# Attention of a two-layer trunk: read-back of turned blocks, residual loads, closing normalisation and two copies moved

## The chip, the cores and the metric

The kernel runs on one core of a Trainium2 chip. The time is that of one whole execution in device microseconds. A core has five engines that work side by side, each on its own list of instructions in order: TensorE (PE in the profile, with PEld for its weight loads), VectorE (DVE), ScalarE (ACT), GpSimd (POOL) and SyncE (SP), which here issues the transfers between DRAM and the core's memory. Engines wait for one another by semaphores. Matrix products go to PSUM, from where VectorE and ScalarE fetch them; everything else lies in SBUF.

## The reference, cut to what matters

```python
def diff_attention(qkv, q_gain, k_gain, lam_params, sub_gain, lam_init):
    q, k, v = jnp.split(qkv, 3, axis=-1)                 # 8 heads, two parts r of 64 each, values of 128
    q = rms_norm(q.reshape(bsz, seq, 8, 2, 64), q_gain) * (64 ** -0.5)
    k = rms_norm(k.reshape(bsz, seq, 8, 2, 64), k_gain)
    ...
    logits = einsum('bqhrd,bkhrd->bhrqk', q_blk, k) - slopes * dist    # causal
    probs = softmax(logits)
    attn = probs[:, :, 0] - lam * probs[:, :, 1]
    o = einsum('bhqk,bkhe->bqhe', attn, v)
    ...
    o = rms_norm(o, sub_gain) * (1.0 - lam_init)

def reference(...):                                      # SEQ = D_MODEL = 1024, fp32
    for layer in range(2):
        if layer == 0: h = h + even_mixer(h)             # gMLP gate and gated delta rule
        else:          h = h + diff_attention(rms_norm(h) @ w_qkv) @ w_out
        h = h + square(relu(rms_norm(h) @ w_mlp1)) @ w_mlp2
        h = h + (p[layer] @ w_ple_proj) * sigmoid(rms_norm(h) @ w_ple_gate)
```

The change touches the attention of the second layer and the output projection behind it, and nothing else.

## The kernel before, in words

Every product is made of fp32r parts: an operand is split into a high and a low part (`hi`, `lo`), and `mm3` (L206) multiplies high by high, high by low and low by high. The tile framework puts the written program into an order for each engine by its own model of durations, readiness and priority, and sets the semaphores. `Ordered` (L44) adds to that: `behind` (L60) tells the framework to place one instruction after another, without a wait on the chip; `mark` is the name of the last matrix instruction written so far.

**Attention** (`attention`, L877). The loop at L1150 runs over 64 blocks `g` = 8 heads times 8 blocks of 128 queries, and two more turns for the rest. In turn `g` it writes `logits(0)` of block `g`, `combine` and `transpose` of block `g-1`, `logits(1)` of block `g`, and `value` of block `g-3`. Between them `pump` (L1126) takes units from the stream that projects q, k and v of the next heads (matrix products `mm`), and behind the 220th pump units of `tails` (L1137): the projected outputs of the heads that are done.

- `logits` (L1015): scores to PSUM (`qk`), VectorE adds the slopes and takes the extreme (L1029), ScalarE takes the exponential (L1032).
- `combine` (L1034): VectorE, the two probabilities into one. `transpose` (L1042): VectorE turns 32x32 squares (L1045), SP writes the block to `a_dram` (L1047) and reads it back with the squares in turned places into `aT` (L1053). The read-back must wait until the write has landed.
- `value` (L1056): `po` = the turned block times v; VectorE copies `po` to `o` (L1064), ScalarE squares it with a sum (L1066); behind every fourth block VectorE, GpSimd (L1078 to L1080) normalise four blocks of `o`, and SP writes them to `o_dram` (L1082).
- `put_q` (L985): for each of the two parts `r`, ScalarE scales 64 rows of the turned queries out of PSUM (L993), VectorE copies these to the other 64 rows (L994), and VectorE makes the low part (L995). `put_k` (L975) does the like for the keys.
- `put_o` (L1084): four outputs are turned on PE (`tr`), ScalarE makes `ohi` (L1090) and VectorE `olo` (L1091).

PSUM has tags of two buffers each: `mm`, `tr`, `aux`, `sc`. `tr` serves `put_k`, `put_q` and `put_o`; in the projection behind the attention `mm` and `tr` both take products.

**Projection.** `mix_part` (L1186) multiplies the first six (first half of the tokens) or five heads (second half) by `w_out`, one of eight tiles `m` of 128 outputs after another. It loads the residual row `res` (L1193), makes the products, adds `res` (L1199) and stores the sum in `h_dram` (L1200). `res` comes from `tmp`, a ring of four buffers of 128x512 that the squares of the attention use too. `mix_out` (L1203) does the rest with the remaining heads: load of `acc` from `h_dram` (L1214), products, sum (L1225), squares (L242, L243), store (L1227).

**Close.** The last block's `value` and the last `put_o` stand in `close` (L1179), which the caller runs at the 8th of 16 steps of `mix_out(0)` (L1950). The upper half of `acc` for the first tokens (tiles 4 to 7) lies where v of the last heads lay, so its load waits for the last `po`.

Of the kernel before, what the change touches and what calls it, by code (L numbers as in the profile page):

```python
# [39 lines left out]
def f32(ap):  # L40
    return ap.bitcast(F32)
# [73 lines left out]
class Trunk:  # L115
# [761 lines left out]
    def attention(self, w_qkv, w_out, gain_next, h_dram):  # L877
# [91 lines left out]
        def begin(hd):  # L969
# [15 lines left out]
            def put_q(b2):  # L985
                pt = self.aux([P, HT], "tr", "tr")
                for i in range(2):
                    self.pe.transpose(pt[:, i * P : (i + 1) * P], qk[0][b2 // 2][:, 2 * (b2 % 2) + i, :], self.ident)
                qh = self.slot(f"c{11 + b2 % 2}", [P, 2, 2 * P], F32R, "qh")
                ql = qlow[b2 % 2]  # L990
                for r in range(2):
                    own, other = half[r], half[1 - r]
                    nc.scalar.activation(qh[own, r], pt[own, 0 : 2 * P], AF.Copy, scale=self.qg[own])  # L993
                    nc.vector.tensor_copy(qh[other, r], f32(qh[own, r]))  # L994
                    nc.vector.scalar_tensor_tensor(ql[own, r], pt[own, 0 : 2 * P], self.qg[own], f32(qh[own, r]), ALU.mult, ALU.subtract)  # L995
                return qh, ql
# [4 lines left out]
        class Block:  # L1001
# [40 lines left out]
            def transpose(me):  # L1042
# [5 lines left out]
                src = a_dram.rearrange("k (i r) (j c) -> k (r j) i c", r=32, c=32)  # L1048
                me.aT = []
                for k0 in range(0, nk, 4):  # L1050
                    k1 = min(nk, k0 + 4)
                    aT = self.attn_tile(next(aT_tag))
                    nc.sync.dma_start(aT[:, : (k1 - k0) * P].rearrange("p (k i c) -> p k i c", i=4, c=32), src[k0:k1].rearrange("k p i c -> p k i c"))  # L1053
                    me.aT.append(aT)

            def value(me):  # L1056
# [7 lines left out]
                nc.vector.tensor_copy(o[b // 4][:, b % 4, :], po)  # L1064
# [85 lines left out]
        for g in range(8 * NB + 2):  # L1150
# [15 lines left out]
            pump()  # L1166
            if g > 2:
                blocks[g - 3].value()
# [10 lines left out]
        def close():  # L1179
            blocks[8 * NB - 1].value()  # L1180
            put_o(7, 1, os[7][1])

        return close


    def mix_part(self, h, n, w_out, h_dram):  # L1186
        nc = self.nc
        cols = slice(h * HT, (h + 1) * HT)
        for m in range(KT):
            if m % 2 == 0:  # L1190
                w = self.weight(w_out[0 : n * P, m * P : (m + 2) * P], n, 256)
            res = self.tmp()
            nc.sync.dma_start(res, h_dram[m, :, cols])  # L1193
# [684 lines left out]
def trunk(tc, x, p, ln_mix_e, w_in_e, gmlp_v_gain, gmlp_ws, gmlp_bs, gdn_conv, gdn_a_log, gdn_dt_bias, gdn_out_gain,  # L1878
          w_out_e, ln_mix_o, w_qkv_o, attn_q_gain, attn_k_gain, diff_lambda, attn_sub_gain, w_out_o, ln_mlp, w_mlp1,
          w_mlp2, ln_ple, w_ple_gate, w_ple_proj, masks, out):  # L1880
    with ExitStack() as ctx:
# [54 lines left out]
        for layer in range(2):  # L1936
# [10 lines left out]
            if layer:  # L1947
                T.new_hs()
                for n, _ in enumerate(T.mix_out(0, lambda m: acc_of(m, 0), w_out_o[0], h_dram, gain[4], KA[0])):
                    if n + 1 == 4 * (KT - KA[0]):  # L1950
                        close()
# [11 lines left out]
            close = T.attention(w_qkv_o[0], w_out_o[0], gain[4], h_dram)  # L1963
# [41 lines left out]
```

## Time and profile before

| | us |
|---|---|
| time, median of 3 runs | 2525.89 (2522.48 to 2528.98) |
| the profiled execution, its own time | 2526.67 |
| its span, first to last instruction | 2524.9 |
| mean granted TensorE clock | 0.996 |
| attention and both halves of its projection lie at | 1260 to 1800 of the span |

The profile counts from the start of the span. It gives the busy time of each engine, a table by stretch (busy us of each engine with the number of instructions, the granted TensorE clock as a share of full speed, the share of the transfer engines and GB/s), the waits by who waited for whom, and a timeline. The busy time of PE is pipelined and its ends are modelled, so a row of the timeline with an idle time and its releaser is the surest sign of a wait on PE.

### The profile page before, as it was taken

What the parts mean: (1) busy time and instruction counts of PE and PEld (TensorE: products, weight loads), DVE (VectorE), ACT (ScalarE), POOL (GpSimd) and SP (SyncE); (2) the same over time, 40 slices, a digit from 0 to 9 for tenths busy, and PEclk for the clock granted to TensorE, in tenths of its full rate; (3) what the DMA queues carried; (4) which work ended last, traced back from release to release, by engine and by line L of the source; (5) the groups of instructions that cost most, each with busy time, mean ns of one, the idle gap of its engine ahead of it and who ended that gap; (6) DMA issues with size and microseconds to landing.
All of it is one profiled execution on the core that took longest, in us unless ns stands there. A gap on an engine that the chain in (4) does not pass through costs nothing.

```text
span 2524.9 us, 39928 instructions
## 1 busy us (share of the span) xinstructions
PE 2493.6 (99%) x13758; PEld 2126.0 (84%) x13758; DVE 1899.0 (75%) x3740; ACT 1246.7 (49%) x2457; POOL 287.5 (11%) x256
## 2 busy tenths in 40 slices
PE   9999999999999999999999999999999999999999
PEld 7898898888888887888999999977788888888877
DVE  7876767587667879566588888986887677787586
ACT  6543444465455435444355555543654445445452
POOL 0211232000000000000244343300000000000000
PEclk9999999999999999999999999999999999999999
DMA  7353435447556755553346666779375558655651
GB/s 241 123 161 80 133 110 186 142 163 245 168 179 233 253 185 194 186 167 106 111 119 159 159 167 144 180 214 292 127 230 199 173 189 283 209 188 184 199 179 59
DMA packets 494531, 443.06 MB, mean 175 GB/s; under 512 B 188436, under 2 KB 361464, under 8 KB 494328
## 3 DMA queue, kind: packets, MB, share of 16 engines
q1 hardware_dynamic: 494312, 440.51, 56.8%
q8 instruction: 108, 1.77, 0.3%
q14 instruction: 95, 0.78, 0.1%
q10 hardware_dynamic: 16, 0.00, 0.0%
HBM read 312.47 MB, written 127.93 MB: 174 GB/s over the span
## 4 chain that ended last, share of the span: by engine, by line
PE 85%; DVE 8%; DMA 4%; issue 2%; SPq 1%; ACT 1%; POOL 0%; DVEq 0%; ACTq 0%; POOLq 0%
PE mm L76 75%; PE aux L76 2%; PE po L76 2%; PE qk L76 2%; DVE lg L1029 1%; DMA raw<-in_w_mlp_dram 1%; PE tr L79 1%; DVE lg L1040 1%; DVE w L224 1%; DVE lg L1045 1%; DMA raw<-in_w_ple_gate_dram 1%; DVE ks L983 0%; DVE ql L995 0%; DMA aT<-a_dram 0%; DVE ss L921 0%
## 5 line engine op out<-in xcount | busy, mean ns | idle before, releaser
L76 PE MATMUL mm<-g,w 128*128 128x512 f32 x2592 | 603.7, 394 | 0.8 <-DVE g L224 0.5
L223 ACT CAST w<-raw 128x512 fp32r<-128x512 f32 x598 | 365.7, 618 | 455.3 <-PE mm L76 370.5
L76 PEld LDWEIGHTS mm<-g,w 128*128 128x128 f32 x2592 | 485.9, 188 | 116.3 <-issue 1.1
L76 PE MATMUL mm<-hi,w 128*128 128x512 f32 x1728 | 554.6, 397 | 0.3 <-ACT hi L1240 0.3
L76 PE MATMUL mm<-w,hi 128*128 128x256 f32 (+2 forms) x2528 | 502.3, 295 | 0.9 <-DVE k L928 0.7
L224 DVE TENSOR_TENSOR w<-raw,w 128x512 fp32r<-128x512 f32 x534 | 364.3, 690 | 180.5 <-ACT w L223 176.1
L76 PEld LDWEIGHTS mm<-w,hi 128*128 128x128 f32 x2528 | 399.2, 188 | 15.1 <-PE qk L76 0.6
L76 PEld LDWEIGHTS mm<-hi,w 128*128 128x128 f32 x1728 | 325.3, 189 | 73.9 <-ACT hi L1240 0.7
L76 PE MATMUL mm<-w,lo 128*128 128x256 f32 (+2 forms) x1264 | 369.5, 293 | 0.0
L76 PE MATMUL mm<-lo,w 128*128 128x512 f32 x864 | 342.0, 396 | 0.9 <-DVE lo L1241 0.9
L76 PE MATMUL mm<-t,w 128*128 128x512 f32 x1152 | 270.9, 394 | 1.2 <-ACT w L223 1.2
L76 PEld LDWEIGHTS mm<-t,w 128*128 128x128 f32 x1152 | 216.2, 188 | 52.8 <-ACT w L223 1.6
L76 PEld LDWEIGHTS mm<-w,lo 128*128 128x128 f32 x1264 | 238.1, 188 | 6.1
L76 PEld LDWEIGHTS mm<-lo,w 128*128 128x128 f32 x864 | 163.2, 189 | 37.0 <-DVE lo L1241 1.4
L224 DVE TENSOR_TENSOR g<-graw,g 128x512 fp32r<-128x512 f32 x216 | 147.3, 686 | 8.0 <-DMA gd<-g 7.0
L223 ACT CAST g<-graw 128x512 fp32r<-128x512 f32 x216 | 132.9, 618 | 30.1 <-issue 9.3
L1032 ACT ACTIVATE lg<-lg,nm 128x128 f32<-128x128 f32 (+7 forms) x128 | 99.6, 778 | 84.1 <-DVE nm L1029 83.1
L260 POOL TENSOR_TENSOR r<-ms,mhalf 128x4 f32<-128x4 f32 x12 | 13.4, 1119 | 1043.1 <-DVE ms L258 1015.3
L350 ACT ACTIVATE g<-g 128x512 f32<-128x512 f32 x96 | 60.6, 633 | 112.5 <-DVE g L284 109.0
L224 POOL TENSOR_TENSOR w<-raw,w 128x512 fp32r<-128x512 f32 x64 | 84.6, 1337 | 99.6 <-ACT w L223 67.9
L76 PE MATMUL mm<-ohi,w 128*128 128x512 f32 x256 | 89.7, 413 | 3.9 <-DVE t L1199 2.4
L76 PE MATMUL mm<-ahi,w 128*128 128x512 f32 x256 | 82.8, 399 | 0.4 <-DVE acc L1225 0.4
(334 smaller groups left out, 3551.2 us busy)
## 6 DMA issues: line engine op xcount, KB each, us to landing
raw<-in_w_mlp_dram SPq DMA_DIRECT2D x352, 256.0 KB, 3.2
graw<-gd SPq DMA_DIRECT2D x224, 256.0 KB, 2.7
gd<-g SPq DMA_DIRECT2D x192, 256.0 KB, 3.0
raw<-in_w_ple_gate_dram SPq DMA_DIRECT2D x76, 256.0 KB, 3.0
acc<-h_dram SPq DMA_DIRECT2D x64, 256.0 KB, 4.4
keep<-in_w_mlp_dram SPq DMA_DIRECT2D x64, 256.0 KB, 4.1
raw<-in_w_in_e_dram SPq DMA_DIRECT2D x60, 256.0 KB, 3.6
h_dram<-acc SPq DMA_DIRECT2D x48, 256.0 KB, 2.6
```

What stands on the lines that cost most here:

```text
L76: self._next(self.engine.matmul(*a, **k))
L79: self._next(self.engine.transpose(*a, **k))
L223: self.nc.scalar.copy(hi, src)
L224: (lo_engine or self.nc.vector).tensor_tensor(lo, src, f32(hi), ALU.subtract)
L260: nc.gpsimd.tensor_tensor(r, ms, self.mhalf[:, 0:4], ALU.pow)
L350: nc.scalar.activation(g, src, AF.Relu)
L1029: nc.vector.tensor_tensor_reduce(out=lg[:, k0:k1], in0=ps[:, : k1 - k0], in1=al[:, u0 + k0 : u0 + k1], scale=-1.0, scalar=3.0e38 if c == 0 ...
L1032: nc.scalar.activation(lg[:, :n], lg[:, :n], AF.Exp, bias=nm[:, r, nch - 1 : nch], scale=-1.0, accum_out=me.sums[:, b, r : r + 1])
L1040: nc.vector.scalar_tensor_tensor(me.lg[1][:, :n], me.lg[1][:, :n], rs, me.lg[0][:, :n], ALU.mult, ALU.add)
L1045: nc.vector.transpose(me.lg[0][:, :n], me.lg[1][:, :n])
```

## The change

Four edits in the attention and its projection:

1. In `put_q` the copy to the other 64 rows is made by ScalarE, straight from PSUM with the same scale, in place of VectorE's copy in SBUF.
2. In `value` the copy of `po` to `o` is made by ScalarE in place of VectorE.
3. The read-back of `aT` becomes a method `fetch` that the loop calls behind `logits(1)` of the next block, and each read is placed behind the last matrix instruction written until then.
4. `mix_part` loads the residual row of tile `m+1` ahead of the products of tile `m`. `close` is split: `value` at the 8th step of `mix_out(0)`, `put_o` at the 12th.

```diff
@@ put_q @@
                     nc.scalar.activation(qh[own, r], pt[own, 0 : 2 * P], AF.Copy, scale=self.qg[own])
-                    nc.vector.tensor_copy(qh[other, r], f32(qh[own, r]))
+                    nc.scalar.activation(qh[other, r], pt[own, 0 : 2 * P], AF.Copy, scale=self.qg[own])
                     nc.vector.scalar_tensor_tensor(ql[own, r], pt[own, 0 : 2 * P], self.qg[own], f32(qh[own, r]), ALU.mult, ALU.subtract)
@@ transpose @@
-                src = a_dram.rearrange("k (i r) (j c) -> k (r j) i c", r=32, c=32)
+                me.src = a_dram.rearrange("k (i r) (j c) -> k (r j) i c", r=32, c=32)
+
+            def fetch(me):
+                nk = me.b + 1
                 me.aT = []
                 for k0 in range(0, nk, 4):
                     k1 = min(nk, k0 + 4)
                     aT = self.attn_tile(next(aT_tag))
-                    nc.sync.dma_start(aT[:, : (k1 - k0) * P].rearrange("p (k i c) -> p k i c", i=4, c=32), src[k0:k1].rearrange("k p i c -> p k i c"))
+                    self.pe.behind(nc.sync.dma_start(aT[:, : (k1 - k0) * P].rearrange("p (k i c) -> p k i c", i=4, c=32), me.src[k0:k1].rearrange("k p i c -> p k i c")), self.pe.mark)
                     me.aT.append(aT)
@@ value @@
-                nc.vector.tensor_copy(o[b // 4][:, b % 4, :], po)
+                nc.scalar.copy(o[b // 4][:, b % 4, :], po)
                 sq = self.tmp(P)
                 nc.scalar.activation(sq, po, AF.Square, accum_out=me.osq[:, b : b + 1])
@@ attention, the loop and its end @@
                 blocks[g].logits(1)
             pump()
+            if 0 < g <= 8 * NB:
+                blocks[g - 1].fetch()
             if g > 2:
                 blocks[g - 3].value()
...
-        def close():
-            blocks[8 * NB - 1].value()
-            put_o(7, 1, os[7][1])
-
-        return close
+        return blocks[8 * NB - 1].value, lambda: put_o(7, 1, os[7][1])
@@ mix_part @@
+        def load(m):
+            if m < KT:
+                res = self.tmp()
+                nc.sync.dma_start(res, h_dram[m, :, cols])
+                return res
+
+        ahead = load(0)
         for m in range(KT):
             if m % 2 == 0:
                 w = self.weight(w_out[0 : n * P, m * P : (m + 2) * P], n, 256)
-            res = self.tmp()
-            nc.sync.dma_start(res, h_dram[m, :, cols])
+            res, ahead = ahead, load(m + 1)
             ps = self.mm_ps()
@@ trunk @@
-                    if n + 1 == 4 * (KT - KA[0]):
-                        close()
+                    if n + 1 in (4 * (KT - KA[0]), 6 * (KT - KA[0])):
+                        close.pop(0)()
...
-            close = T.attention(w_qkv_o[0], w_out_o[0], gain[4], h_dram)
+            close = [*T.attention(w_qkv_o[0], w_out_o[0], gain[4], h_dram)]
```

The framework orders each engine anew. The lists below hold line, operation, what is written, what is read, and the shape; the number behind a name tells one buffer use from another.

**SP, the second call of `mix_part`, by the write of the last block (`a_dram_18841`).** The residual row of tile 4 is `t_19002` before and `t_18955` now, that of tile 5 `t_19022` and `t_19004`. Before:

```order
L101 DMA raw_19227<-in_w_out_o_dram 128x512
L1214 DMA acc_19360<-h_dram 128x512
L101 DMA raw_19342<-in_w_out_o_dram 128x512
L1214 DMA acc_19360<-h_dram 128x512
L1047 DMA a_dram_18841<-lg_12530 128x8x128
L1200 DMA h_dram<-t_18933 128x512
L101 DMA raw_19348<-in_w_out_o_dram 128x512
L1193 DMA t_19002<-h_dram 128x512
L1193 DMA t_19022<-h_dram 128x512
```

Now:

```order
L101 DMA raw_19218<-in_w_out_o_dram 128x512
L1194 DMA t_18955<-h_dram 128x512
L101 DMA raw_19342<-in_w_out_o_dram 128x512
L1222 DMA acc_19360<-h_dram 128x512 x2
L1047 DMA a_dram_18841<-lg_12530 128x8x128
L1208 DMA h_dram<-t_18883 128x512
L101 DMA raw_19348<-in_w_out_o_dram 128x512
L1194 DMA t_19004<-h_dram 128x512
```

Tile 4's load stood behind the block's write, a store and a weight load, and now stands ahead of them all; tile 5's has kept its place behind the weight load.

**PE, the close.** `po_19191` is the last value product, `tr_19212` (now `tr_19251`) the turning of the last four outputs, `mm` with `ohi_19105` or `ohi_19123` are products of `mix_out(0)`, with `ohi_18832` or `ohi_19114` of `mix_out(1)`. Before (lines left out are the further products of the same tiles):

```order
L76 MATMUL po_19191<-v_16753,aT_18845 128x128 x4
L76 MATMUL mm_19179<-ohi_19105,w_19129 128x512
...
L76 MATMUL mm_19248<-ohi_19105,w_19223 128x512
...
L76 MATMUL mm_19274<-ohi_19123,w_19230 128x512
L79 MATMUL tr_19212<-ident,o_18817 128x128 x4
L76 MATMUL mm_19235<-ohi_19105,w_19223 128x512
```

Now:

```order
L76 MATMUL po_19191<-v_16753,aT_18894 128x128 x4
L76 MATMUL mm_19226<-ohi_19105,w_19214 128x512
...
L76 MATMUL mm_19179<-ohi_19105,w_19129 128x512
...
L76 MATMUL mm_19239<-ohi_19105,w_19214 128x512
...
L76 MATMUL mm_19274<-ohi_19123,w_19221 128x512
L76 MATMUL mm_19377<-ohi_18832,w_19344 128x512
...
L76 MATMUL mm_19377<-ohi_19114,w_19351 128x512
L79 MATMUL tr_19251<-ident,o_18817 128x128 x4
```

Between the last value product and the turning stood 18 products of 512 columns (three tiles), and now stand 30 (four tiles and six products of a fifth); tile `mm_19179` starts five products later behind `po`.

**PE, the start of the last head.** `tr_18152` turns keys, `tr_18161` queries, `tr_18191` (now `tr_18187`) four outputs of an earlier head; `qk_18175` is the first score product of the head. Before:

```order
L79 MATMUL tr_18152<-ident,k_17746 128x128 x4
...
L79 MATMUL tr_18161<-ident,q_17744 128x128 x2
L76 MATMUL mm_18236<-olo_18147,w_18224 128x512
L76 MATMUL mm_18236<-ohi_18146,w_18225 128x512
L76 MATMUL qk_18175<-ks_18151,qh_18164 128x128
L76 MATMUL qk_18260<-ks_18151,qh_18164 128x256
L76 MATMUL qk_18175<-ks_18151,ql_12526 128x128
L76 MATMUL qk_18260<-ks_18151,ql_12526 128x256
L79 MATMUL tr_18191<-ident,ol_18066 128x128 x4
```

Now:

```order
L79 MATMUL tr_18152<-ident,k_17744 128x128 x4
...
L79 MATMUL tr_18161<-ident,q_17742 128x128 x2
L76 MATMUL mm_18234<-olo_18147,w_18222 128x512
L76 MATMUL mm_18234<-ohi_18146,w_18223 128x512
L76 MATMUL qk_18175<-ks_18151,qh_18164 128x128
L76 MATMUL qk_18262<-ks_18151,qh_18164 128x256
L76 MATMUL mm_18294<-ohi_18072,w_18216 128x512
...
L76 MATMUL mm_18294<-ohi_18146,w_18223 128x512
L76 MATMUL qk_18175<-ks_18151,ql_12526 128x128
L76 MATMUL qk_18262<-ks_18151,ql_12526 128x256
L79 MATMUL tr_18187<-ident,ol_18062 128x128 x4
```

The first score products stand where they stood, two products behind the queries' turning; the twelve products of `mm_18294` have moved ahead of the low parts and of the next turning of outputs.

## The prediction, made before the changed kernel ran

> **What bounds the kernel now.** I read the page's first rows, then the table by stretch around the edited stage, then the waits of PE in it, and last the timeline at the places where PE stands still. The first two rows are the page's; the rest is the table by stretch (start and end, length, busy us of PE, PEld, DVE, ACT, POOL with their instructions, granted clock, share of the transfer engines, GB/s).
>
> ```profile
> span 2524.9 us, 39928 instructions
> PE 2493.6 (99%) x13758; PEld 2126.0 (84%) x13758; DVE 1899.0 (75%) x3740; ACT 1246.7 (49%) x2457; POOL 287.5 (11%) x256
> ...
> 600.00:700.00 100.00, 100.00 (x433) 81.15 (x432) 68.19 (x108) 47.91 (x84) 0.00 (x0) 1.00 0.58 190
> 1260.00:1700.00 440.00, 431.74 (x3285) 411.55 (x3284) 386.75 (x1055) 245.26 (x601) 156.73 (x126) 0.99 0.67 161
> 1300.00:1640.00 340.00, 335.21 (x2662) 324.78 (x2661) 305.70 (x841) 191.90 (x474) 136.17 (x111) 1.00 0.68 159
> 1640.00:1660.00 20.00, 16.54 (x85) 13.34 (x84) 18.09 (x40) 11.15 (x27) 2.65 (x2) 0.83 0.78 204
> 1649.70:1656.60 6.90, 6.10 (x17) 4.91 (x18) 6.74 (x15) 2.70 (x8) 0.00 (x0) 0.51 0.68 113
> 1700.00:1704.00 4.00, 2.69 (x12) 1.49 (x10) 2.84 (x7) 1.20 (x4) 0.00 (x0) 1.00 0.98 302
> 1733.00:1736.00 3.00, 1.51 (x7) 1.19 (x7) 2.16 (x4) 0.00 (x0) 0.00 (x0) 1.00 1.01 284
> 1750.00:1761.00 11.00, 7.08 (x25) 5.58 (x26) 5.43 (x12) 2.33 (x6) 2.25 (x3) 0.84 1.05 394
> 1755.50:1759.00 3.50, 3.43 (x10) 2.90 (x11) 1.39 (x3) 0.69 (x1) 0.02 (x1) 0.51 1.06 401
> ```
>
> PE is the bound: it has something to do in 99% of the span, and in an undisturbed stretch (600 to 700) a product of 512 columns starts every 100/433 = 0.23 us. The change takes nothing from PE, so all that it can gain is the time in which PE stands still in this stage, and what the clock loses behind that. By the rows PE is idle for 340.00 - 335.21 = 4.8 us in the long attention stretch, 20.00 - 16.54 = 3.5 at the start of the last head, 1.3 and 1.5 in the projection, and 11.00 - 7.08 = 3.9 at the close: 15.0 together. Two of these places are followed by a stretch at half clock (0.51), where 6.10 us and 3.43 us of busy PE did about half of that in work: 3.0 and 1.7 lost. The whole stake is 19.7 us, 0.8% of the time.
>
> Who PE waited for in 1260 to 1800 (us in total, times, longest):
>
> ```profile
> PE tr L79 <- POOL o L1080: 2.8, 1, 2.8
> PE mm L76 <- DVE t L1199: 2.4, 2, 1.5
> PE qk L76 <- DVE qh L994: 1.9, 2, 1.4
> PE po L76 <- DMA aT<-a_dram: 1.6, 3, 0.7
> PE mm L76 <- DVE acc L1225: 1.5, 1, 1.5
> ```
>
> The names are those of the four edits: the closing normalisation (L1080), the residual sum (L1199), the query copy (L994), the read-back (`aT`). So each edit aims at a real wait; the question is how much of each it reaches.
>
> **Two copies to ScalarE.** Durations (min/median/max in ns) and, in the last two rows, what ScalarE waited for between 1260 and 1700:
>
> ```profile
> L993 ACT ACTIVATE qh<-tr,qg x64: 454/471/474, 1262.6 to 1690.4; 64x256 fp32r<-64x256 f32 x64
> L994 DVE CAST qh<-qh x64: 284/289/1358, 1263.5 to 1691.1; 64x256 fp32r<-64x256 f32 x64
> L995 DVE SCALAR_TENSOR_TENSOR ql<-tr,qg,qh x64: 435/484/493, 1263.8 to 1691.4; 64x256 fp32r<-64x256 f32 x64
> L1064 DVE COPY o<-po x64: 245/288/294, 1287.6 to 1747.6; 128x128 f32<-128x128 f32 x64
> L1066 ACT ACTIVATE t<-po x64: 257/278/283, 1290.5 to 1751.7; 128x128 f32<-128x128 f32 x64
> ...
> ACT t L1066 <- DVE o L1064: 57.6, 38, 4.1
> ACT qh L993 <- DVE ql L995: 16.4, 21, 1.6
> ```
>
> VectorE loses 64 x 0.289 + 64 x 0.288 = 37 us and falls from 386.75 to about 350 of 440; ScalarE gains 64 x 0.471 + 64 x 0.278 = 48 us and rises from 245 to 293 of 440. Neither becomes the bound by its sum. Much of the 48 us fills time that ScalarE spent waiting: 57.6 us for VectorE's copy of `po` ahead of its own square of the same tile, which now follows a copy on the same engine. For the queries the chain of one part was 0.47 + 0.29 + 0.48 = 1.24 us and becomes 0.47 + 0.47 + 0.48 = 1.42, as the low part now has both ScalarE reads ahead of it; the second part waits for the first one's low part (21 waits), so a turning takes 2.8 us in place of 2.5. Against that, the high part no longer waits in VectorE's queue, the fuller of the two. What hides the longer chain is the products between a turning and its first score product; without that cover each of the 32 turnings costs 0.36 us, 11.5 us in all.
>
> A rule of the Trainium skill speaks against these two edits: the page "ScalarE: Activation LUTs", section "Rules for kernel authors", puts plain elementwise work on VectorE and not on ScalarE. The rows agree on the length of the query copy (0.47 against 0.29), but not for `po` (0.28 against 0.29); by the rule alone the two edits would be a loss, which is the third rival below.
>
> **The read-back.** SP's own waits between 1270 and 1740, and the landing of the `aT` reads:
>
> ```profile
> SPq L1053 <- DMA a_dram<-lg: 115.3, 53, 4.4
> ...
> DMA to landing us min/median/max: 1.9/3.5/6.4
> ```
>
> SP stands for 115 us with a read at its head that waits for its own write; that is what the edit would have to open for other transfers. In the new order of SP the reads stand as near behind their writes as before (2.4 rows on average, 2.6 before): the placing behind a matrix instruction sets an order in the framework's plan and no wait, and there is little else to go between. I cost it at nothing. The cover is the two turns between a block's write and its `value`; only three products waited for `aT`, 1.6 us. Bounds: 1.6 gained, or 4 lost if some `value` that now stands nearer behind its logits meets a landing of 6.4 in place of 3.5 once or twice.
>
> For the stretch 1300 to 1640 I take, of the 4.8 us of idle PE, 0.9 gained: half of the 1.6 for `aT` and of the few tenths for `qh` there. Bounds: 4 lost (above), 4.8 gained.
>
> **The residual rows.** VectorE's waits in 1640 to 1780, its longest, and SP's issues ahead of it:
>
> ```profile
> DVE t L1199 <- DMA t<-h_dram: 16.0, 4, 7.0
> ...
> 1733.84 0.69 DVE L1199 TENSOR_TENSOR t<-t,mm 128x512 f32<-128x512 f32 x1 [6.99 <-DMA t<-h_dram]
> ...
> 1721.92 0.39 SPq L101 DMA_DIRECT2D raw<-in_w_out_o_dram  x1
> ...
> 1727.18 1.13 SPq L1193 DMA_DIRECT2D t<-h_dram  x2
> ```
>
> VectorE works in order, so while it waits 7 us for a row, the weights' low parts and sums behind it wait too. PE stood for this at 1700 to 1704 and 1733 to 1736, 1.3 + 1.5 = 2.8 us. The long one is tile 4 of the second call: its load has moved ahead of the last block's write, a store and a weight load, to a place behind the weight load that was issued at 1721.92 in place of 1727.18, 5 us earlier, which leaves about 2 of VectorE's 7 us and nothing for PE. Tile 5 has hardly moved. The loads hold a second buffer of a ring of four, so a load may now wait for the store two tiles back; a tile lasts 15 products or more (3.5 us), and the load has two tiles. I take 2.3 gained; bounds 2.8, and 1.5 lost if the ring holds a load up once.
>
> **The close.** PE, ScalarE and GpSimd from the last value product on:
>
> ```profile
> 1745.35 1.50 PE L76 MATMUL po<-v,aT 128*128 128x128 f32 x12
> 1751.15 0.50 PE L76 MATMUL mm<-ohi,w 128*128 128x512 f32 x1 [1.52 <-DVE acc L1225]
> 1755.57 1.11 PE L79 MATMUL tr<-ident,o 128*128 128x128 f32 x4 [2.76 <-POOL o L1080]
> ...
> 1751.13 0.63 ACT L242 ACTIVATE t<-acc 128x512 f32<-128x512 f32 x1 [1.20 <-DVE acc L1225]
> 1751.67 0.26 ACT L1066 ACTIVATE t<-po 128x128 f32<-128x128 f32 x1
> ...
> 1754.48 1.04 POOL L1080 TENSOR_TENSOR o<-o,of 128x512 f32<-128x512 f32 x1
> ```
>
> The last `po` ends at 1746.9, the normalised `o` at 1755.5, and PE turns it at 1755.6: 8.7 us, covered by 18 products (18 x 0.23 = 4.1 us) and 1.52 + 2.76 = 4.3 us of waiting. The chain is long because the square of `po` (1751.67) stands in ScalarE's order behind the square of an output tile (1751.13), and it still does in the new order. That tile's products now start five later (1.2 us), which the chain can bear, as VectorE reached its sum 2 us late anyway. So the chain stays 8.7 us, the cover becomes 30 products, 6.9 us, and 1.8 us of waiting are left: 2.5 gained. A lone wait of this size (1733 to 1736) left the clock at 1.00, so the 1.7 us at half clock may go too; I count half, 0.8. Together 3.3. Bounds: 5.6 (all), and 1.5 lost, if the upper `acc` rows, whose load still waits for the last `po`, hold PSUM and stop PE once more.
>
> **The start of the last head.** PE's three waits ahead of the first half-clock stretch:
>
> ```profile
> 1645.07 0.66 PE L79 MATMUL tr<-ident,k 128*128 128x128 f32 x4 [1.06 <-DVE olo L1091]
> 1648.56 0.49 PE L76 MATMUL qk<-ks,qh 128*128 128x128 f32 x2 [1.45 <-DVE qh L994]
> 1650.50 0.87 PE L79 MATMUL tr<-ident,ol 128*128 128x128 f32 x3 [0.94 <-PE qk L76]
> ```
>
> The third goes: twelve products (2.8 us) now stand ahead of that turning. The second changes its name, from VectorE's copy to ScalarE's, two products behind the turning as before; the first hangs on VectorE's queue, which is lighter by a tenth. I take 1.4 of the 3.5 us, and of the 3.0 us at half clock 1.8, as the idle time that brought it on is less than two thirds. Together 3.2; bounds 6.5, and 2 lost.
>
> On the clock a rule of the Trainium skill stands against my reading: "TensorE: Matmul & The Clock Gate", section "HAM oscillation — how this bites in real kernels", asks for gaps of PE above about 3.4 us. The trace differs, as 0.51 followed gaps of 1.06, 1.45 and 0.94. By the page no gap here would touch the clock, the 0.8 and 1.8 fall away, and the time would be 2518.8.
>
> As a mechanism of this kernel that would be half-clock stretches that come whatever the waits do. It ends inside the forecast's own range, and I give it 0.1 of the forecast's chance.
>
> **Sum.** 0.9 + 2.3 + 3.3 + 3.2 = 9.7 us. The profiled execution took 2526.67, 0.8 above the median of 2525.89; 2526.67 - 9.7 = 2517.0, and on the median's scale 2516.2.
>
> **The rivals.** First, everything that the edits aim at goes: 2.8 + 5.6 + 6.5, and 1.6 + 0.5 in the long stretch, 17.0 us, 2508.9. For it: the waits carry the edits' own names. Against: neither the 8.7 us chain nor the first score product has its cover complete.
>
> Second, the waits only change their names: the reads are not later, tile 5's load has kept its place, a turning takes longer, and the clock drops as before. What is left is 2.5 at the close and about 1.1 in the projection: 3.6 us, 2522.3. For it: SP's order by the read-backs, and transfer engines at 0.98 to 1.05 in 1700 to 1761, where a load issued earlier only queues elsewhere.
>
> Third, slower: ScalarE's order becomes the wait. Its two copies of a part stand behind exponentials and casts, and the first score product after a turning waits for `qh`, as it did once for 1.4 us at the last head. If a third to a half of the 32 turnings, say 13, lose those 1.4 us, 18 are lost against 5.6 gained in the projection and at the close: 2538. It decides from ten such turnings on (14 - 5.6 is above 7.6). Against: only 2 of 32 waited in the trace, and ScalarE is idle for a third of the stage even with the copies.
>
> **How the numbers follow.** The forecast has 0.52, its own range 2511 to 2521; first rival 0.16, second 0.21, third 0.11. A measurement of this kernel tells 0.3% (7.6 us) from no change, so faster means below 2518.3: about three quarters of the forecast (0.40) and the first rival, 0.56; same is the rest of the forecast (0.12) and the second, 0.33; slower 0.11. The range reaches from the first rival with the spread of the runs (3 us) halved, 2507, to 4 lost at the read-back with the rest at nothing, 2530; what is left out is most of the third rival and a little below.
>
> **What would show it.** Right: no wait of PE for L1080 above 2 us; VectorE's waits for residual rows at 5 us or less; no stretch of half clock behind the close, and a shorter one or none at the last head; the square of `po` waiting for no VectorE copy; SP's waits for `a_dram` near 115 us. Wrong: waits of `qk` for ScalarE's `qh` of more than 5 us; waits for `aT` above 4 us; 0.5 clock at other places of the stage; PE idle in 1300 to 1640 above 8 us.

## The result, and the profile after

| | before | changed |
|---|---|---|
| median of 4 runs, us | 2525.62 (2522.48 to 2528.98) | 2512.74 (2511.04 to 2515.96) |
| ratio, 95% interval | | 0.9950 (0.9933 to 0.9968) |
| the profiled execution, us | 2526.67 | 2514.11 |

The changed kernel is 12.9 us faster, 0.5%. The page's first rows:

```profile
span 2512.4 us, 39957 instructions
PE 2487.6 (99%) x13758; PEld 2122.9 (84%) x13758; DVE 1862.2 (74%) x3612; ACT 1288.0 (51%) x2585; POOL 287.1 (11%) x256
```

The table by stretch, columns as in the prediction:

```profile
1300.00:1640.00 340.00, 337.95 (x2688) 328.41 (x2686) 284.64 (x758) 229.39 (x581) 136.92 (x112) 0.99 0.70 166
1300.00:1620.00 320.00, 319.79 (x2572) 312.65 (x2571) 265.83 (x714) 217.02 (x554) 131.12 (x107) 1.00 0.70 164
1630.00:1645.00 15.00, 12.82 (x68) 10.09 (x67) 14.47 (x29) 10.49 (x21) 1.90 (x1) 0.89 0.89 236
1636.60:1640.00 3.40, 3.40 (x12) 2.56 (x11) 3.34 (x8) 2.35 (x6) 1.90 (x1) 0.53 1.06 353
1725.00:1735.00 10.00, 8.94 (x46) 7.16 (x45) 3.63 (x6) 2.18 (x4) 0.00 (x0) 1.00 0.95 276
1735.00:1750.00 15.00, 9.53 (x35) 6.86 (x34) 10.00 (x19) 6.33 (x13) 2.25 (x3) 0.89 1.02 376
```

The stretch 1300 to 1620 ends ahead of the last head's start in both kernels. Its row in the kernel before:

```profile
1300.00:1620.00 320.00, 315.21 (x2506) 305.59 (x2505) 287.20 (x787) 180.49 (x448) 130.98 (x106) 1.00 0.68 159
```

In the same 320 us PE now makes 2572 products in place of 2506. At 320/2572 = 0.124 us each the 66 are 8.2 us, nearly twice the 4.8 us that PE shows as idle before. VectorE's busy time falls from 90% to 83%.

The starts of the products, which are not modelled, give the same loss. From the first score product to the 313th of 384, with 2733 products of PE between them in both kernels, it took 348.2 us and now takes 339.9: 8.3 us. All of it lies in steps of more than 0.3 us from one start to the next: 29 of them with 13.5 us before, 16 with 5.2 us now, while the shorter steps add up to 334.7 and 334.6. So these are a few stops, and each costs more than it shows as idle, because a product is drawn longer than the step to the next one: the page has a mean of 295 ns for products of the name `mm<-w,hi`, the most common ones in this stretch, and the median step from one of them to the next product is 118 ns here.

Where PE waits now, between 1250 and 1800:

```profile
PE mm L76 <- ACT t L242: 3.7, 1, 3.7
PE tr L79 <- DVE olo L1094: 1.8, 1, 1.8
PE mm L76 <- DVE acc L1233: 1.7, 1, 1.7
PE mm L76 <- DVE t L1207: 1.1, 2, 0.9
...
PE po L76 <- DMA aT<-a_dram: 0.4, 2, 0.2
PE qk L76 <- ACT qh L994: 0.3, 1, 0.3
```

The wait for GpSimd's `o` is gone, but the waits at the close are longer together (3.7 for `t` and 1.7 for `acc`, 5.4 us) than they were (2.8 for `o` and 1.5 for `acc`, 4.3 us). The timeline at the close, SP first, then VectorE, ScalarE and PE:

```profile
1719.74 5.27 SPq L1056 DMA_DIRECT2D aT<-a_dram  x2
...
1726.25 0.42 SPq L1194 DMA_DIRECT2D t<-h_dram  x1
...
1738.07 2.71 SPq L1222 DMA_DIRECT2D acc<-h_dram  x5
```

```profile
1729.36 0.69 DVE L1207 TENSOR_TENSOR t<-t,mm 128x512 f32<-128x512 f32 x1 [4.70 <-DMA t<-h_dram]
...
1743.10 1.36 DVE L1233 TENSOR_TENSOR acc<-acc,mm 128x512 f32<-128x512 f32 x2 [2.10 <-DMA acc<-h_dram]
```

```profile
1736.84 0.25 ACT L1067 COPY o<-po 128x128 f32<-128x128 f32 x1
...
1743.88 1.25 ACT L242 ACTIVATE t<-acc 128x512 f32<-128x512 f32 x2 [3.83 <-DVE acc L1233]
```

```profile
1731.62 1.05 PE L76 MATMUL po<-v,aT 128*128 128x128 f32 x8
...
1739.19 0.50 PE L76 MATMUL mm<-ohi,w 128*128 128x512 f32 x1 [1.72 <-DVE acc L1233]
...
1744.61 0.47 PE L76 MATMUL mm<-ohi,w 128*128 128x512 f32 x1 [3.75 <-ACT t L242]
```

The last `po` ends at 1732.7. The upper `acc` rows, whose tile it held until then, are issued at 1738.07, behind stores and loads in SP's order; VectorE sums them at 1743.10, and the PSUM tiles that these sums empty stop PE for 3.75 us. The row names ScalarE's squares, but these stood 3.83 us for the same sums. The close's wait has moved from the normalisation to those rows.

A yardstick that does not hang on modelled ends is the start of an instruction. The first score product, the last value product and the end of the span cut the stage in two: A, the attention with most of the projection, and B, all behind the last value product.

| | first `qk` | last `po` | span | A | B |
|---|---|---|---|---|---|
| before | 1273.1 | 1746.6 | 2524.9 | 473.5 | 778.3 |
| changed | 1271.9 | 1732.4 | 2512.4 | 460.5 | 780.0 |

A is 13.0 us shorter, B 1.7 us longer, and 1.2 us were won ahead of the attention, where nothing was changed. Both kernels have 3399 products of PE in A and 3368 in B. The 1.2 us are scatter: the first `qk` starts between 1270.7 and 1273.1 in the fourteen kernels that are compared below.

### The profile page after: what moved, and what is told of

It is laid out like the page before. It is cut to its first block, busy times and chain, and to the rows that moved or that the text cites. A ratio compares the mean times of both kernels' runs of the same rounds, so it can differ in the third digit from the quotient of the medians.

```text
span 2512.4 us, 39957 instructions
## 1 busy us (share of the span) xinstructions
PE 2487.6 (99%) x13758; PEld 2122.9 (84%) x13758; DVE 1862.2 (74%) x3612; ACT 1288.0 (51%) x2585; POOL 287.1 (11%) x256
## 3 DMA queue, kind: packets, MB, share of 16 engines
q1 hardware_dynamic: 494312, 440.51, 57.6%
## 4 chain that ended last, share of the span: by engine, by line
PE 94%; DMA 2%; DVE 2%; issue 1%; ACT 0%; SPq 0%; POOL 0%; DVEq 0%; ACTq 0%; POOLq 0%
PE mm L76 81%; PE po L76 3%; PE qk L76 3%; PE aux L76 2%; PE tr L79 1%; DMA raw<-in_w_mlp_dram 1%; DMA acc<-h_dram 0%; PE pz L76 0%; PE py L76 0%; PE pvn L76 0%; DVE w L224 0%; DMA a_dram<-lg 0%; PE aux L79 0%; PE pab L79 0%; PE pkq L76 0%
## 5 line engine op out<-in xcount | busy, mean ns | idle before, releaser
L76 PEld LDWEIGHTS mm<-w,hi 128*128 128x128 f32 x2528 | 399.9, 188 | 13.9
L1032 ACT ACTIVATE lg<-lg,nm 128x128 f32<-128x128 f32 (+7 forms) x128 | 99.3, 776 | 74.8 <-DVE nm L1029 73.9
L1029 DVE CUSTOM_DVE_ANT_0 lg<-qk,al 128x512 f32<-128x512 f32 (+3 forms) x128 | 74.7, 587 | 23.1 <-PE qk L76 18.3
```

Of the source, the lines that this page charges most:

```text
L76: self._next(self.engine.matmul(*a, **k))
L1029: nc.vector.tensor_tensor_reduce(out=lg[:, k0:k1], in0=ps[:, : k1 - k0], in1=al[:, u0 + k0 : u0 + k1], scale=-1.0, scalar=3.0e38 if c == 0 ...
L1032: nc.scalar.activation(lg[:, :n], lg[:, :n], AF.Exp, bias=nm[:, r, nch - 1 : nch], scale=-1.0, accum_out=me.sums[:, b, r : r + 1])
```

## The experiments

Twelve kernels, five rounds each, beside the kernel before on the same chip: its median was 2526.45 beside e1 to e4, 2525.37 beside e5 to e8 and 2525.28 beside e9 to e12. A, B and the last column are from one execution of each kernel. Read together:

| run | median, us | ratio to before (95%) | A | B | products and VectorE busy us in 1300 to 1620 |
|---|---|---|---|---|---|
| changed | 2512.74 | 0.9933 to 0.9968 | 460.5 | 780.0 | 2572, 265.8 |
| e1 both copies alone | 2512.76 | 0.9936 to 0.9962 | 461.0 | 777.6 | 2574, 265.9 |
| e2 changed, without copies | 2524.18 | 0.9982 to 0.9999 | 471.2 | 780.6 | 2505, 286.7 |
| e3 copy of `po` alone | 2524.72 | 0.9984 to 1.0001 | 471.7 | 777.7 | 2512, 282.6 |
| e5 query copy alone | 2519.78 | 0.9963 to 0.9985 | 467.8 | 777.3 | 2535, 278.5 |
| e6 changed, with idle copies | 2526.78 | 0.9997 to 1.0015 | 478.3 | 775.3 | 2445, 288.0 |
| e4 upper rows in a free tile | 2515.73 | 0.9940 to 0.9967 | 457.9 | 783.6 | 2569, 265.6 |
| e7 short stores | 2512.80 | 0.9934 to 0.9962 | 459.9 | 776.5 | 2568, 265.5 |
| e8 MLP loads later | 2513.68 | 0.9939 to 0.9965 | 459.7 | 780.6 | 2572, 265.4 |
| e9 copies, close, free tile | 2512.57 | 0.9939 to 0.9964 | 461.3 | 777.9 | 2562, 264.9 |
| e10 last read-back on GpSimd | 2511.16 | 0.9935 to 0.9960 | 459.5 | 777.7 | 2576, 265.6 |
| e11 e10 and free tile | 2511.68 | 0.9933 to 0.9961 | 463.3 | 774.1 | 2569, 265.5 |
| e12 e9 and last read-back | 2510.01 | 0.9930 to 0.9955 | 462.2 | 773.4 | 2569, 265.6 |

A and B hold the same products in all of them but four: in e4 and e9 five products of the projection more stand behind the last value product, in e11 six fewer, in e12 two fewer (0.23 us each, so 1.2, 1.4 and 0.5 us pass from one column to the other). Executions of one kernel lie 4 us and more apart (2509.99 to 2516.73 for e7), so a difference of 2 us in A or B is a hint and no more.

### Which edit: the copies alone, and all but the copies

The kernel before with edits 1 and 2:

```diff
-                    nc.vector.tensor_copy(qh[other, r], f32(qh[own, r]))
+                    nc.scalar.activation(qh[other, r], pt[own, 0 : 2 * P], AF.Copy, scale=self.qg[own])
...
-                nc.vector.tensor_copy(o[b // 4][:, b % 4, :], po)
+                nc.scalar.copy(o[b // 4][:, b % 4, :], po)
```

> The kernel before with the two copies on ScalarE and nothing else. Theory (VectorE relieved): the stretch 1300 to 1640 lost about 9 us more than its products need before and 1 us after, because VectorE ran behind PE; the copies alone bring 7 to 10 us there and at the last head, so about 2517 against 2525.6, and VectorE's waits for PE's score products rise from 6.7 us to about 19 as in the changed kernel. Rival A (the read-back that is issued later in SP's order did it): 2524 or more here. Rival B (no single edit, the framework's plan happened to fall better): anything between, with the lost time in other places than before.

The changed kernel with these lines turned back:

> The changed kernel with both copies back on VectorE. Theory (VectorE relieved): about 8 us come back, 2520 to 2523, as small gaps of PE between 1300 and 1640, and ScalarE waits over 50 us for VectorE's copy of po again. Rival A (read-back): 2514 or less, the stretch stays free of gaps. Rival B (plan): no fixed value, but no 50 us wait is needed for a loss.

The copies alone reach 2512.76, the whole gain and 4 us more than their theory had; without them 2.3 us are left by the medians, 0.3 to 4.5 by the interval (0.9982 to 0.9999). Where PE waits with the copies alone, and its table row:

```profile
PE tr L79 <- POOL o L1080: 3.2, 1, 3.2
PE tr L79 <- DVE olo L1091: 1.8, 1, 1.8
PE mm L76 <- DVE t L1199: 1.7, 2, 1.2
PE qk L76 <- ACT qh L994: 1.1, 1, 1.1
```

```profile
1300.00:1620.00 320.00, 320.00 (x2574) 313.05 (x2574) 265.92 (x713) 216.77 (x554) 131.66 (x107) 1.00 0.71 164
```

The long stretch has no idle PE at all; the waits at the close still have the names of before. The read-back (rival A) is out: with it, the residual rows and the close, but without the copies, the gaps come back: 2505 products, and ScalarE waits 58.7 us for VectorE's copy of `po` as before (57.6).

### Which copy, and by its time or by who waits for it

The copy of `po` alone:

> The kernel before with only the copy of po on ScalarE (18 us of VectorE's work moved, and ScalarE's square no longer behind VectorE). If the relief is by the work taken from VectorE, this half brings about half, 3 to 5 us, 2521 to 2523. If it is the wait of the square for VectorE's copy, which holds the PSUM tile and ScalarE's queue, it brings nearly all, 2516 to 2519. If the query copy ahead of the score products is what matters, nothing: 2525.

The query copy alone:

> The kernel before with only the copy of the query's high part on ScalarE; the copy of po stays on VectorE. The copy of po alone brought nothing beyond 2 us. Theory A (the query's chain matters: score products of a new pair of blocks wait for it and the copy stood in VectorE's queue): this brings nearly all, 2513 to 2516. Theory B (VectorE's load matters and has a threshold: 18 us of relief are not enough, 37 are): this brings about as little as the other copy alone, 2521 to 2525, with the same small gaps of PE between 1300 and 1640.

The changed kernel with as many copies put back on VectorE, of the mask row onto itself, for which no one waits:

```diff
                     nc.scalar.activation(qh[other, r], pt[own, 0 : 2 * P], AF.Copy, scale=self.qg[own])
+                    nc.vector.tensor_copy(al[own, 0 : 2 * P], al[own, 0 : 2 * P])
...
                 nc.scalar.copy(o[b // 4][:, b % 4, :], po)
+                nc.vector.tensor_copy(al[:, 0 : 2 * P], al[:, 0 : 2 * P])
```

> The changed kernel, to which VectorE gets as many copies as it lost, at the same places of the program, but of its own mask row onto itself, so that nothing waits for them and they wait for nothing of another engine. Theory B (load): the gaps of PE between 1300 and 1640 come back, 7 us or more of them, and the time rises to 2520 to 2525. Theory A (it is who waits for the copies, not the time they take): the stretch stays free of gaps, 2512 to 2515.

By the medians the copy of `po` alone brings 1.7 us (none to 4.0 by the interval), the query copy 5.6 (3.8 to 9.3), and the two together 13.7 (9.6 to 16.2). So for the copy of `po` the third of its expectations came true, nothing, and the wait of ScalarE's square for that copy, which went with it, is not what cost the time; the query copy fell between its two theories (2513 to 2516, 2521 to 2525) and met neither. For the idle copies the theory of load holds: the time is 2526.78, not told apart from the kernel before (0.9997 to 1.0015), and 2 us above what that theory had. Its row, and what ScalarE waits for:

```profile
1300.00:1620.00 320.00, 310.59 (x2445) 301.37 (x2444) 288.03 (x768) 204.20 (x527) 127.74 (x102) 0.99 0.66 152
```

```profile
ACT lg L1033 <- DVE nm L1030: 105.5, 67, 4.3
```

VectorE is busy for 288.0 of 320 us again, PE makes 127 products fewer than in the changed kernel, and the exponentials wait 105.5 us for VectorE's extremes (73.9 in the changed kernel, 83.1 before). A fixed stretch holds more work where PE is faster, so the kernels are better compared over the same work, from the first score product to the 313th, with 2733 products of PE between them in each:

| run | time for the same products, us | VectorE busy in it, us | share |
|---|---|---|---|
| before | 348.2 | 309.7 | 89% |
| e2 changed, without copies | 348.5 | 309.5 | 89% |
| e3 copy of `po` alone | 347.8 | 304.8 | 88% |
| e5 query copy alone | 344.6 | 295.8 | 86% |
| e1 both copies alone | 340.1 | 278.8 | 82% |
| changed | 339.9 | 278.8 | 82% |
| e6 changed, with idle copies | 356.9 | 314.8 | 88% |

The more VectorE has to do for the same products, the longer they take. At 86% there is still a loss of 4.7 us against the changed kernel, at 82% PE shows 0.2 us of idle time; where between the two the loss begins was not tried. That the copy of `po` brings little fits: its 51 instructions fewer take only 4.9 us off VectorE's busy time here, the query copies 13.9.

The idle copies do not show that any work on VectorE costs as much. They stand at the old places, the query ones ahead of the low part `ql`, and ScalarE keeps its two copies of each part, so the chain of a turning is longer than in the kernel before. PE's longest named waits in 1300 to 1640 are of that chain: 2.5 and 2.2 us for ScalarE's `qh` and 1.8 for `ql`. How much of the loss is load and how much that chain was not separated; both run through VectorE's order. This, beside the greater work, may be why the run lies behind the kernel before in this table.

The idle copies cost VectorE more than what was taken from it. Of 1260 to 1700, the copies of the kernel before, and the idle ones (count, then busy us and mean ns, then idle time ahead):

```profile
L994 DVE CAST qh<-qh 64x256 fp32r<-64x256 f32 x64 | 22.9, 358 | 3.0 <-ACT qh L993 1.1
L1064 DVE COPY o<-po 128x128 f32<-128x128 f32 x59 | 16.8, 285 | 1.2 <-PE po L76 0.3
```

```profile
L995 DVE COPY al<-al 64x256 f32<-64x256 f32 x56 | 22.7, 406 | 0.5
L1069 DVE COPY al<-al 128x256 f32<-128x256 f32 x56 | 19.7, 352 | 0.2
```

39.7 us for 123 copies before, 42.4 us for 112 here. One reason stands in the last section.

### The close: bytes, order on SP, or the upper rows

The upper rows of `acc` in a tile that is free before the last value products:

```diff
-        return self.rp.tile(shape, dt, tag=tag, name=self.nm(name))
+        return self.rp.tile(shape, dt, tag=self.swap.get(tag, tag), name=self.nm(name))
...
             close = [*T.attention(w_qkv_o[0], w_out_o[0], gain[4], h_dram)]
+            T.swap = {"A1": "A5", "A5": "A1"}
```

> The changed kernel with the accumulator's upper rows of the first half (tiles 4 to 7) in the region of the last probability rows, which is free before the last value products, in place of that of the values, which is not; the MLP's later tiles change places with it. Theory (at the close PE now waits for these rows: loads issued at 1738.07, sums at 1743.10, PE held 3.75 us): the 3.75 us and about half of the 1.7 us at half clock go, 4 to 5 us, about 2508. Rival (the normalisation of the last outputs is as late, and GpSimd's o takes over as the wait): 0 to 1.5 us, 2511 to 2513.

The stores of the projection cut short, to 64 of 512 columns; the rest of these rows is left out, so the outputs are not those of the reference:

```diff
-            nc.sync.dma_start(h_dram[m, :, cols], a)
+            few = slice(h * HT, h * HT + 64) if k0 else cols
+            nc.sync.dma_start(h_dram[m, :, few], a[:, 0 : few.stop - few.start])
```

> The changed kernel, with the stores of the second attention's output rows cut to 64 of 512 columns (3.5 MB less to move between 1730 and 1770; the order and the number of transfers are as before, the rows that are read later are left incomplete). Beside their nominal pace the products lose 11 to 12 us between 1705 and 1820 in every kernel so far (11.7 before, 11.8 after, 12.9 with the rows in the free tile). Theory T (the transfer engines are full there, 0.98 to 1.06, and set the pace, so a wait removed comes back under another name): 3 to 6 us less, 2507 to 2510. Theory O (the order on SP, in which loads stand behind stores that wait for VectorE, sets it): within 1.5 us of the changed kernel.

The MLP's first weight loads placed later:

```diff
-                nc.sync.dma_start(out[i], w1[...])
+                inst = nc.sync.dma_start(out[i], w1[...])
+                if last and c < 2:
+                    self.pe.behind(inst, self.rb_mark)
```

> The changed kernel, with the first eight weight loads of the MLP (2 MB, now issued between the projection's own transfers from 1729 on) placed behind the last products of the projection's first half. Theory T (transfer engines full): the 2 MB take about 5 us of them, which go to the residual and accumulator rows; 3 to 5 us less, 2508 to 2510. Theory O (order on SP): the rows still stand behind the stores, 0 to 2 us less, and up to 3 us more if the MLP's first products then wait for their weights.

All three were misses for the theory named first. The free tile (2509.84 to 2520.55) missed its rival as well, and the other two are where their rival, SP's order, put them. With the free tile the wait for the upper rows went, and PE waits for a residual row in its place:

```profile
PE mm L76 <- DVE t L1208: 3.8, 2, 3.4
PE tr L79 <- POOL o L1084: 2.3, 1, 2.3
```

With the short stores the transfer engines are less full at the close (0.57 in 1740 to 1760 against 0.83 in the changed kernel), and the median is the same to 0.1 us. So the bytes of the stores are not what holds the close. Their rows, of the changed kernel and of the short stores:

```profile
1740.00:1760.00 20.00, 16.25 (x70) 13.02 (x69) 14.27 (x26) 8.36 (x15) 3.64 (x4) 0.91 0.83 291
```

```profile
1740.00:1760.00 20.00, 17.44 (x81) 14.10 (x82) 15.60 (x28) 9.40 (x16) 3.74 (x4) 1.00 0.57 174
```

The next four ask for SP's order. e9 is the kernel before with both copies, the split close and the free tile. e10 is the changed kernel with the last block's read-back on another queue, e11 that with the free tile, and e12 is e9 with that read-back:

```diff
-                    ... nc.sync.dma_start(aT[...], ...)
+                    ... (nc.gpsimd if 8 * me.hd + me.b > 62 else nc.sync).dma_start(aT[...], ...)
```

> The kernel before with the two copies, the last outputs' transposition two tiles later (as in the change) and the upper accumulator rows in the free tile; without the read-back's new place and without the residual rows loaded ahead. With the copies alone PE waited 3.2 us for GpSimd's o and VectorE 3.9 us for the upper rows. Theory Q (the residual rows loaded ahead hold two of four temporaries and are what the free tile's kernel lost to, 3.4 us in one wait for t): 3 to 5 us below the copies alone, 2508 to 2510. Theory S (SP standing 5 us at the last read-back, with residual rows queued behind it, is what is left in every variant): within 2 us of the copies alone, 2511 to 2514.

> The changed kernel with the last block's read-back (2 of 96 reads) issued on GpSimd's queue, where nothing is waiting at that time, in place of SP's. In the changed kernel SP stands 5.3 us at this read (1719.74 to 1725.10) for its own write, and the residual rows of the last two tiles are issued behind it; VectorE then waits 4.7 and 2.0 us for them, and ScalarE's copy of the last po stands behind it. Theory S: SP no longer stands there, the two rows come 3 to 5 us earlier, and 3 to 5 us go, 2508 to 2510. Theory T (the transfer engines' bytes, already without support from the shortened stores) or the upper rows' loads, which wait for the last value products: 0 to 1.5 us.

> The run before this one with the upper accumulator rows in the free tile as well, so that neither of the two loads stands behind what it need not wait for. Theory S: 4 to 8 us below the changed kernel, 2505 to 2509, and PE's loss beside its nominal pace between 1705 and 1820 falls from 12 to 5 to 7 us. If only one of the two loads decides, no better than the better of the two alone.

> The kernel before with the two copies, the later transposition, the upper rows in the free tile and the last read-back on GpSimd's queue; without the read-backs' new place in SP's order and without residual rows ahead. If those two edits of the change bring nothing of their own, this equals the run before it, 2505 to 2509; if the residual rows ahead bring the 2 us that were predicted of them, this is 2 us slower than it.

e9 is where theory S put it, e10 where its rival did (1.6 us, within the spread). e11 missed its 2505 to 2509 by 3 us and is no better than e10; e12 equals it within the spread, so the reads' new place and the residual rows ahead bring nothing that these runs can tell. Who PE waits for in e10, and in e12:

```profile
PE tr L79 <- POOL o L1083: 2.8, 1, 2.8
PE tr L79 <- DVE olo L1094: 1.8, 1, 1.8
```

```profile
PE tr L79 <- POOL o L1081: 2.1, 1, 2.1
PE tr L79 <- DVE olo L1092: 1.8, 1, 1.8
PE mm L76 <- DVE t L1196: 1.4, 1, 1.4
```

The wait is GpSimd's `o` again: where the upper rows or the residual rows were eased, another of the three chains was the next to be waited for. B is lowest where all are eased at once (773.4 and 774.1, against 778.3 before), but 0.5 and 1.4 us of that are products that passed to A, and e6, with the close of the changed kernel, has 775.3. e12 has the lowest median, 2510.01, but its interval overlaps that of the changed kernel; it also leaves out edit 3 and the residual rows ahead and loses nothing by it against e11. What would have to go for the rest of the close's waits stays open.

## Why the prediction was right, and where it was not

The forecast of 2516.2 was 3.5 us too high, inside its own range of 2511 to 2521. That its sum held is luck: the long stretch brought 7.3 us more than forecast and the close 4.8 less. By the rows above, against the profiled execution:

| term | predicted | measured | from |
|---|---|---|---|
| long attention stretch | 0.9 | 8.2 | 66 products |
| start of the last head | 3.2 | 2.7 | 6.5 - 3.8 |
| residual rows | 2.3 | 1.3 | PE's waits for `t`, 2.4 to 1.1 |
| close | 3.3 | -1.5 | 5.6 - 7.1 |
| ahead of the attention | 0 | 1.2 | first `qk` |

Together 11.9 of the 12.56 us. The terms are differences of one execution each. At the last head the 3.8 are 15.00 - 12.82 = 2.2 us of idle PE and 1.6 lost in 3.40 us at 0.53; at the close the 7.1 are 15.00 - 9.53 = 5.5 and 0.11 x 15 = 1.6 by the clock of 0.89.

- **Long attention stretch: the step that failed.** "I take, of the 4.8 us of idle PE, 0.9 gained" mis-sized it by 7 us, beyond its own bound of 4.8. The working took the relief of VectorE only as far as a wait carried the name of a copy (`qh`), and took the idle time of PE as all there was to win. The runs show that VectorE at 90% was itself the wait, under the name of whatever it was late with (`k` 0.7 us, `nm` 1.1, `qh` 0.5), that the copies alone win it, and that idle copies for which no one waits bring the loss back. The 37 us taken from VectorE were worked out, but used only to show that it was not the bound.
- **Last head: right in size, but not by the clock.** The wait for VectorE's copy (1.4 us) went, and half clock shortened from 6.9 to 3.4 us. The copies alone show the same wait for `olo`, 1.8 us, so none of it is due to the other edits. But the 1.6 us charged to the clock are not lost: e7 has the same order there, ran 1630 to 1645 at 1.00, waited 1.1 us for ScalarE's `qh` in place of 0.3, and its 361st score product starts 402.3 us behind the first, against 402.4 in the changed kernel. VectorE is busy for 14.47 of these 15 us, so it is likely that VectorE sets the pace there.
- **Read-back at nothing: not contradicted.** No run has this edit alone. Without the copies (e2) PE's waits for `aT` are 5.0 us in place of 1.6, so it may cost something there. SP's waits for `a_dram` even rose:

```profile
SPq L1056 <- DMA a_dram<-lg: 138.9, 53, 4.9
```

- **Residual rows: right for the tile that was looked at, half the size in PE's waits.** VectorE's wait for tile 4's row (7.0 us) went altogether. The longest is now 4.7 us for tile 6, behind SP's 5.27 us at the last read-back; it was 4.56 us before, and the working did not look at it. What was won does not reach the end: e12 does without it.
- **Close: wrong, at its lower bound.** The step was that the later start of that tile is something "which the chain can bear" and that "1.8 us of waiting are left"; the bound named the upper `acc` rows, and these it was in the profiled execution. With B as the yardstick the changed kernel and e2 lie 2.3 to 2.4 us above their partners without edits 3 and 4 (780.0 against 777.6, 780.6 against 778.3), a difference that one execution of each makes likely and does not show; the medians of the changed kernel and of the copies alone are the same.
- **Signs.** Of those named, no wait for the normalised `o`, 5 us or less for the residual rows, a shorter half clock at the last head, and the square of `po` free of VectorE came true; no half clock behind the close did not (0.89 in 1735 to 1750), and SP's waits for `a_dram` were 138.9 us and not near 115. None of the four signs against it appeared: `qh` 0.3 us, `aT` 0.4 us, 2.0 us of idle PE in 1300 to 1640.
- **Rivals.** The third (ScalarE's order becomes the wait) fell: ScalarE is busy 295.6 us of 1260 to 1700 in place of 245.3, and PE waits 0.3 us for its `qh` (1.1 in the copies alone). The first (2508.9) ended almost as near as the forecast, on the other side, but by the copies and not by the close it counted on. The second (waits only change their names) holds for the close, not for the attention.

The rule of the Trainium skill that was weighed against the copies ("ScalarE: Activation LUTs", "Rules for kernel authors") would have made this a loss; the two copies alone won 13.7 us by the medians. Another of its pages, "Perfetto Trace Analysis", section "Optimizing Scalar/DVE Operations", says that work may well move from VectorE to ScalarE where VectorE is saturated. The trace agrees with that one: the stretch was at 90%, and 64 copies of 0.47 us on ScalarE in place of 0.29 us still paid.

## What to carry to other kernels

An engine that works in order at 90% in the stretch can be a wait with many names, and taking work from it can win more than the rows with the moved instruction's name show, and more than the bound engine shows as idle (8.3 us against 4.8 here). So compare the time that the bound engine takes from one instruction to another with the same number between them. Copies for which no one waits, put on the engine in question, show whether its time or the waiting for a result costs, but only for the place where they stand. Where several chains end close to each other, as at the close here, easing one of them brought nothing that these runs could tell, and easing all of them 1.1 and 2.7 us by the medians, with intervals that overlap.

## What the runs showed of the hardware

**VectorE's copies within SBUF wait for GpSimd.** The query copy has a median of 289 ns and a maximum of 1358. VectorE, and then GpSimd, in the kernel before:

```profile
1560.52 1.10 DVE L994 CAST qh<-qh 64x256 fp32r<-64x256 f32 x1
...
1332.81 1.36 DVE L994 CAST qh<-qh 64x256 fp32r<-64x256 f32 x1
```

```profile
1560.43 1.04 POOL L1080 TENSOR_TENSOR o<-o,of 128x512 f32<-128x512 f32 x1
...
1331.39 2.63 POOL L224 TENSOR_TENSOR w<-raw,w 128x512 fp32r<-128x512 f32 x2 [7.03 <-ACT w L223]
```

The first copy started 0.09 us behind GpSimd's operation and ended 0.15 us behind its end (1561.62 and 1561.47), the second ended at 1334.17 and GpSimd at 1334.02. Seven of the 64 query copies took more than 0.32 us; all seven started while a GpSimd operation ran, and ended 0.14 to 0.15 us behind its end. None of the 41 that started with GpSimd idle took so long; 16 started beside a GpSimd operation and were not held. The idle copies, which are of the same kind, took up to 1378 ns (min/median/max):

```profile
L995 DVE COPY al<-al x56: 243/291/1378, 1310.2 to 1670.6; 64x256 f32<-64x256 f32 x56
```

The copies of `po` out of PSUM never more than 294. The Trainium skill's page "SBUF — State Buffer", section "Who interferes with whom", has this as a lock on ports that VectorE and GpSimd share; the trace agrees. So the query copy cost VectorE more than its median, which is one reason why it was worth more to move than the copy of `po`.

**The clock does not follow the length of one wait.** Behind a wait of 3.2 us the copies alone fell to 0.83 in the 10 us around it, the copy of `po` alone stayed at 1.00 behind one of 3.2 us as well:

```profile
1740.00:1750.00 10.00, 7.68 (x29) 6.21 (x30) 5.22 (x9) 3.09 (x5) 2.10 (x3) 0.83 0.87 324
```

```profile
1740.00:1760.00 20.00, 15.08 (x72) 11.33 (x71) 12.36 (x23) 7.96 (x17) 2.25 (x3) 1.00 1.02 352
```

At the last head the changed kernel fell to 0.89 in 1630 to 1645, and e7, with the same order of products there, stayed at 1.00. What decides it was not tried.
